# First feed-forward stage's down product in seven-product groups, with the last S5 layer's operators built earlier

## The chip, the cores and the metric

The kernel runs on one core of a Trainium2 chip. The metric is the device time of one execution in microseconds (us), lower is better. TensorE (PE) does the matrix products, VectorE (DVE) and ScalarE (ACT) the elementwise work, GpSimd (POOL) a little arithmetic and the issue of some transfers, SyncE (SP) the issue of most transfers.

## What is computed

A trunk of four layers over one sequence of 512 rows by 1024 columns, all in float32. Each layer adds a mixer and then a feed-forward network (FFN) to the running sum `x`, each on a normalised copy of it:

```python
for layer in range(4):
    h = rmsnorm(x, norm_mix[layer])
    # layers 0 and 3: S5 (a diagonal state space), 1: gated linear attention, 2: differential attention
    x = x + mixer[layer](h)
    h = rmsnorm(x, norm_ffn[layer])
    g, u = split(h @ w_gate_up[layer])          # 1024 x 5632
    x = x + (silu(g) * u) @ w_down[layer]       # 2816 x 1024
return rmsnorm(x, norm_final)
```

Float32 products are made of three passes of a rounded float32 format: each operand is split into a high part and the remainder, and high x high, high x low and low x high are summed.

The S5 layer works with *operators* (small matrices that take 16 inputs of a group into 64 states, and states to outputs) and *phases* (cosines and sines), both computed from the layer's parameters alone. So the last S5 layer's operators and phases can be made at any earlier time. They are: made in pieces beside other work, written ("spilled") to DRAM, and read back in layer 3.

## The kernel before

The order of work is: first S5 layer (`s5_first`, ending in its gate and output products, `s5_glu`), FFN 0, linear attention (`gla`), FFN 1, differential attention (`diff`), FFN 2, last S5 layer (`s5_second`), FFN 3.

**Products.** The FFN's gate and up product (`seven_block`) is done in 11 blocks of 256 hidden columns, each as seven products of half-size matrices in place of eight (Strassen's scheme). The down product has two forms. `gemm_b` is the direct one: for each pair of 128-row weight slices and each of four row tiles it issues three 128x512 matmuls (`mm3`, lines 510 to 512). `seven_down` does four blocks at once with seven half-size products (matmuls at line 384), with more splitting and adding on DVE and ACT. FFN 1, 2 and 3 do their 11 blocks in groups of 4, 4 and 3, the first two by `seven_down`, the last by `gemm_b`. FFN 0 alone does groups of 3, 3, 3 and 2, all four by `gemm_b`.

**Jobs.** `gemm_b` with `jobs=True` calls `job()` after each three matmuls. This advances a Python generator by one step, which emits a few instructions of side work. Their place in the program is tied behind the latest weight split and the latest matmul. In FFN 0 the generator is `s5_spilled`: in eight rounds `kk` = 0 to 7 it loads parameters (`s5_loads`), multiplies complex numbers on DVE (`cross`, lines 1508 to 1510), transposes and multiplies small matrices on PE (`s5_qt` line 1554, `s5_xts` line 1655, `s5_rows` line 1621), copies on ACT, shuffles a map through DRAM (`s5_map`, lines 1637 and 1646), and spills three tiles per round (lines 1777 to 1779). All its transfers go through POOL's queue (`self.dq = nc.gpsimd`). A round takes 17 steps. Its tiles lie in the normalised input's memory, which the other FFNs use as weight slots once the opening is over; FFN 0 therefore has two slots of its own more and only three activation buffers (`na = 3`).

The phases (`s5_phases_spilled`, eight steps a round, DVE and ACT only, and one spill) and small tables for the differential attention (`diff_tables`, 13 steps) are jobs of the linear attention's output product (32 steps) and of the last down groups of FFN 1 (16 steps) and FFN 2 (the rest).

**Order.** Most stages are ordered by a list scheduler that takes instructions in program order where its cost model finds them ready. Some stretches are fixed in program order for all engines: `hand_all()` in `gemm_b` begins one at the last four weight slices of the last product of a stage (the tail), and it lasts until the opening of the next FFN (a plan written out in `ffn`) is over. Weight loads go through SP's queue in order, the accumulating loads ("plus") through POOL's.

**Memory.** The FFN and attention pools reuse the same addresses. A tile's first write waits for everything that used the older tiles at its addresses. `edge` tiles only shift addresses. `gate` in `s5_glu` has a ring of 6 x 2048 bytes per partition at the start of the pool.

Of the kernel before, what the change touches and what calls it, by code (L numbers as in the profile page):

```python
# [22 lines left out]
P = 128  # L23
D = 1024
# [370 lines left out]
class Trunk:  # L395
# [578 lines left out]
    def ffn(self, l, left, after=None, turn=False, aside=None, small=None):  # L974


        jobs = bool(aside or small)
        if small:
            self.calls = 16 if l == 1 else -1
# [4 lines left out]
        with self.tc.tile_pool(name=f"ffn{l}", bufs=1, reuse_waits="tile") as fp:  # L984

            na = 3 if aside else 4
# [6 lines left out]
            slots = [fp.tile([P, 4, 256], F32, name=f"slot{n}") for n in range(SLOTS + 2 * (4 - na))]  # L993
# [11 lines left out]
            halved = () if aside else (0, 1)  # L1005
# [66 lines left out]
            for nb in (4, 4, 3) if na == 4 else (3, 3, 3, 2):  # L1072
# [45 lines left out]
                if small:  # L1118
                    self.place = lambda kk: Slices(*slots[2 * (kk % 2) : 2 * (kk % 2) + 2])
# [6 lines left out]
                for d in range(2):  # L1126
                    tail = 4 if d == 1 and b0 + nb == 11 else 0
                    self.gemm_b(stat, wd, 2 * nb, d * 512, self.add_x(d, nxt, r), k0=2 * b0, tail=tail, jobs=bool(aside) or small and not d,
# [3 lines left out]
                    if small and not d:  # L1132
                        self.closed() if l == 1 else list(self.jobs)
# [5 lines left out]
            list(self.jobs) if l == 0 else None  # L1139
# [572 lines left out]
    def s5_spilled(self, pool, L):  # L1712


        nc = self.nc
        inm = pool.tile([P, 2, 4, 64], F32, name="inmsp")
# [5 lines left out]
        self.spill = [{} for _ in range(8)]  # L1722
        self.dq = nc.gpsimd
        raw = self.s5_loads(pool, L, 0, 4)
# [6 lines left out]
        yield  # L1731
        nxt = operators(0, self.s5_qt(raw[1]))
        for kk in range(8):
# [7 lines left out]
            yield  # L1741
            two()
            if kk < 7:
                raw = self.s5_loads(pool, L, 4 * kk + 4, 4)
            yield
# [4 lines left out]
            yield  # L1750
            q_two()
            yield
            yield
            yield
            if kk == 0:
                yield
                yield
                yield
            both = self.tp("cps")
            if kk < 7:  # L1760
                ps = self.s5_qt(raw[1], both)
# [3 lines left out]
            if kk:  # L1765
                yield
            nc.scalar.copy(inm, xs)
            yield
            if kk:
                yield  # L1770
            self.s5_map(L, 4 * kk, 4, rv, rs, mp, True)
            if kk:
                yield
            if kk < 7:
# [6 lines left out]
            yield  # L1781
# [541 lines left out]
    def s5_glu(self, L, zT, accs, after):  # L2323
# [5 lines left out]
        with self.tc.tile_pool(name=f"s5g_{L}", bufs=1) as p:  # L2329
            for d in range(2):  # L2330
                gate = [None] * NT

                def evac_b(t, ps):
                    gate[t] = p.tile([P, 512], F32, tag="gate", name="gate", bufs=6)
# [30 lines left out]
    def gla(self, l, left, after):  # L2365
# [5 lines left out]
        with self.tc.tile_pool(name="gla", bufs=1, reuse_waits="tile") as p:  # L2371
# [369 lines left out]
    def diff_tables(self):  # L2741
# [8 lines left out]
        p = Slices(self.wp.tile([P, 2048], F32, tag="whl", name="dtab", bufs=5))  # L2750
# [484 lines left out]
    def small(self):  # L3235
        yield from self.diff_tables()
# [53 lines left out]
```

## Time and profile before

| | us |
|---|---|
| median of three runs | 2193.45 (2191.31 to 2194.58) |
| the profiled execution's own time | 2192.53 |
| its span, first to last instruction | 2190.8 |
| PE busy in the span | 2131.8 (97%) |
| DVE busy | 1768.2 (81%) |
| ACT busy | 1198.3 (55%) |
| POOL busy | 383.2 (17%) |
| first S5 layer's gate and output products | 139.0 to 206.75 |
| FFN 0 | 206.75 to 564.83 |
| linear attention's output product | 719.34 to 770.09 |
| FFN 1 | 770.09 to 1102.17 |
| FFN 3 | 1861.20 to 2183.29 |

The stages' limits are the starts of their first matmuls. PE busy is the time in which at least one matmul was under way; a matmul's own time (0.39 us for 128x512) is longer than the spacing of two in a row, since they overlap. PEld is the load of the stationary operand, which overlaps the matmuls too. "POOLq" and "SPq" are the queues from which transfers are issued. An arrow names what ended a wait.

### The profile page before, as it was taken

The page shows a single profiled execution, that of the slowest core. Times are in us where ns is not written, and L with a number is a line of the kernel's source. Part 1 is how long each engine was busy: PE and PEld are TensorE (multiplying, and loading weights), DVE is VectorE, ACT ScalarE, POOL GpSimd, SP SyncE. Part 2 cuts the span into 40 slices and gives each one's busy share as a digit, 9 for nine tenths or more (in the row PEclk, how much of TensorE's full clock was granted, in tenths as well). Part 3 has the DMA queues.
Part 4 walks back from the last instruction along what each step waited for, and adds up shares of the span by engine and source line. Part 5 has one row for each costly group of instructions (what it writes and reads, how often), then busy time and mean ns, then how long its engine had stood idle before and what let it go on. Part 6 is the DMA issues. An engine that isn't in the chain of part 4 may idle for free. (4 is left out here: it accounts for less than half of the span.)

```text
span 2190.8 us, 38556 instructions
## 1 busy us (share of the span) xinstructions
PE 2131.8 (97%) x15241; PEld 1936.7 (88%) x15241; DVE 1768.2 (81%) x2644; ACT 1198.3 (55%) x1874; POOL 383.2 (17%) x486
## 2 busy tenths in 40 slices
PE   6999999999999999999999999999999999999998
PEld 5888989989988899999887888989998888989997
DVE  9965978786887799888785786998987974998985
ACT  8634645444665565455555786654555333655553
POOL 3401151431211111111012231111110000111100
PEclk9999999999999999999999999999999999999999
DMA  4356667774863678986477565998862556799852
GB/s 93 66 176 173 177 164 188 172 185 129 208 161 97 188 189 221 222 202 164 143 218 135 114 156 144 246 241 213 204 165 81 153 153 153 191 228 229 203 141 77
DMA packets 328278, 370.40 MB, mean 169 GB/s; under 512 B 71716, under 2 KB 254144, under 8 KB 327970
## 3 DMA queue, kind: packets, MB, share of 16 engines
q1 hardware_dynamic: 246626, 253.68, 38.0%
q0 software_dynamic: 81472, 114.26, 28.3%
q8 instruction: 120, 1.97, 0.4%
q14 instruction: 60, 0.49, 0.1%
HBM read 333.93 MB, written 18.75 MB: 161 GB/s over the span
## 5 line engine op out<-in xcount | busy, mean ns | idle before, releaser
L482 DVE TENSOR_TENSOR whl<-wst,whl 128x1024 fp32r<-128x1024 f32 x240 | 292.0, 1223 | 143.5 <-ACT whl L474 142.2
L656 PE MATMUL a<-side,whl 128*128 128x256 f32 x3240 | 393.9, 278 | 6.7 <-DVE whl L482 4.2
L656 PEld LDWEIGHTS a<-side,whl 128*128 128x128 f32 x3240 | 380.3, 189 | 9.8 <-DVE whl L482 5.7
L474 ACT CAST whl<-wst 128x1024 fp32r<-128x1024 f32 x240 | 251.2, 1051 | 186.6 <-PE acc L512 79.7
L656 PE MATMUL c<-side,whl 128*128 128x256 f32 x2160 | 260.5, 277 | 1.0 <-DVE whl L482 0.7
L656 PEld LDWEIGHTS c<-side,whl 128*128 128x128 f32 x2160 | 252.5, 188 | 1.5 <-DVE whl L482 1.1
L482 DVE TENSOR_TENSOR whl<-slot,whl 128x1024 fp32r<-128x1024 f32 x132 | 160.7, 1223 | 53.0 <-ACT whl L474 52.7
L474 ACT CAST whl<-slot 128x1024 fp32r<-128x1024 f32 x132 | 138.4, 1052 | 106.4 <-DVE slot L912 46.1
L474 ACT CAST whl<-halves 128x1024 fp32r<-128x1024 f32 x111 | 116.2, 1051 | 85.8 <-DVE halves L912 31.5
L482 DVE TENSOR_TENSOR whl<-halves,whl 128x1024 fp32r<-128x1024 f32 x111 | 135.2, 1222 | 18.9 <-ACT whl L474 18.4
L384 PE MATMUL a<-whl,part 128*128 128x512 f32 x576 | 134.7, 389 | 0.0
L656 PE MATMUL a<-sides,whl 128*128 128x256 f32 x1080 | 132.2, 278 | 1.0 <-DVE whl L482 1.0
L656 PE MATMUL d<-sides,whl 128*128 128x256 f32 x1080 | 131.3, 278 | 0.0
L656 PEld LDWEIGHTS a<-sides,whl 128*128 128x128 f32 x1080 | 128.0, 188 | 2.0 <-DVE whl L482 1.2
L656 PEld LDWEIGHTS d<-sides,whl 128*128 128x128 f32 x1080 | 127.6, 188 | 0.2 <-DVE whl L482 0.2
L384 PEld LDWEIGHTS a<-whl,part 128*128 128x128 f32 x576 | 107.6, 188 | 22.3 <-issue 0.3
L510 PE MATMUL acc<-whl,act 128*128 128x512 f32 x320 | 126.4, 395 | 0.9 <-ACT whl L474 0.4
L512 PE MATMUL acc<-whl,act 128*128 128x512 f32 x320 | 125.1, 391 | 0.0
L511 PE MATMUL acc<-whl,act 128*128 128x512 f32 x320 | 125.0, 390 | 0.0
L837 POOL DMA_DIRECT2D wst<-in_ffn_w_gate_up_dram x44 | 57.0, 1296 | 256.4 <-DVE whl L482 66.8
L510 PE MATMUL acc<-whl,zT 128*128 128x512 f32 x192 | 75.5, 393 | 0.0
L511 PE MATMUL acc<-whl,zT 128*128 128x512 f32 x192 | 74.9, 390 | 0.0
(610 smaller groups left out, 4463.0 us busy)
## 6 DMA issues: line engine op xcount, KB each, us to landing
wst<-in_ffn_w_gate_up_dram SPq DMA_DIRECT2D x88, 512.0 KB, 6.4
wst<-in_ffn_w_down_dram SPq DMA_DIRECT2D x70, 512.0 KB, 5.0
slot<-in_ffn_w_gate_up_dram SPq DMA_DIRECT2D x63, 512.0 KB, 5.7
halves<-in_ffn_w_gate_up_dram SPq DMA_DIRECT2D x45, 512.0 KB, 5.7
wst<-in_ffn_w_gate_up_dram POOLq DMA_DIRECT2D x44, 512.0 KB, 7.2
wst<-in_s_w_glu_dram SPq DMA_DIRECT2D x32, 512.0 KB, 4.5
slot<-in_ffn_w_gate_up_dram POOLq DMA_DIRECT2D x24, 512.0 KB, 8.4
wst<-in_diff_w_qkv_dram SPq DMA_DIRECT2D x22, 512.0 KB, 4.9
```

Of the source, the lines that this page charges most:

```text
L384: self.tr.last["mm"] = self.tr.nc.tensor.matmul(banks[t][:], row(y, k, t), hl[:, z, k % 2], start=first and not (k or n), stop=k == 3 and ...
L474: self.last["high"] = self.nc.scalar.copy(hl[:, 0], w[:])
L482: self.last["low"] = self.nc.vector.tensor_tensor(hl[:, 1], w[:], hl[:, 0].bitcast(F32), op=ALU.subtract)
L510: mm(out, lh, rh, start=first, stop=False)
L511: mm(out, lh, rl, start=False, stop=False)
L512: self.last["mm"] = mm(out, ll, rh, start=False, stop=last)
L656: mm(o, *two, start=first and not (j or k or n), stop=k == 3 and n == 2, skip_group_check=True,)
L837: nc.gpsimd.dma_start(w[:], left.quarter(*plus, b), accum_op=ALU.add)
```

## The change

FFN 0 takes the form of the other three: groups of 4, 4 and 3 blocks, four activation buffers, the first two groups by `seven_down`, and the normalised input's memory as weight slots. It has no operator jobs. Its last group has 16 steps of phase jobs (rounds 0 and 1) beside the first half of its down product.

The operators' rounds 0 to 5 become jobs of the three products in the first S5 layer's `s5_glu` (32, 32 and 16 possible steps), in a tile `made` behind an edge of 12352 bytes; one `gate` tile is taken first, so that the ring lies ahead of the edge. Rounds 6 and 7 become jobs of the first half of the linear attention's output product, in two side tiles that its blocks have finished with. In its second half come 8 steps of phases (round 2), in the third side tile. FFN 1's last group gets the tables and then phases (29 steps, rounds 3 and 4), FFN 2's the remaining rounds.

`s5_spilled` itself: a round takes 9 steps, five empty steps come before the first, and its loads, the write of the map and half of the map's reads move from POOL's queue to SP's. With `jobs=True` in `s5_glu` and in the attention's second half, `gemm_b` also emits each weight load and split one pair of slices ahead.

```diff
-    def ffn(self, l, left, after=None, turn=False, aside=None, small=None):
+    def ffn(self, l, left, after=None, turn=False, small=None, calls=-1):
...
-            na = 3 if aside else 4
+            na = 4
...
-            halved = () if aside else (0, 1)
+            halved = (0, 1)
...
-            if aside:
-                self.jobs = aside(Slices(left.whole, left.g))
-            else:
+            if True:
                 slots[:] = [F[0], F[1], slots[0], F[2], left.g[:].rearrange("p (k n) -> p k n", n=256), F[3]] + slots[1:]
...
-            for nb in (4, 4, 3) if na == 4 else (3, 3, 3, 2):
+            for nb in (4, 4, 3):
...
                 if small:
-                    self.place = lambda kk: Slices(*slots[2 * (kk % 2) : 2 * (kk % 2) + 2])
+                    self.place = lambda kk: Slices(own[kk % 2], own[2][:, 2 * (kk % 2) : 2 * (kk % 2) + 2])
+                    self.jobs, self.calls = small, calls
...
     def s5_spilled(self, pool, L, kks):
...
-        self.dq = nc.gpsimd
-        raw = self.s5_loads(pool, L, 0, 4)
+        self.dq = nc.sync
+        raw = self.s5_loads(pool, L, 4 * kks[0], 4)
...
-        yield
-        nxt = operators(0, self.s5_qt(raw[1]))
-        for kk in range(8):
+        for _ in range(5):
+            yield
+        nxt = operators(kks[0], self.s5_qt(raw[1]))
+        for kk in kks:
...
# s5_glu
+            gates = [p.tile([P, 512], F32, tag="gate", name="gate", bufs=6)]
+            if L == 0:
+                self.edge(p, 12352)
+                self.spill = [{} for _ in range(8)]
+                self.jobs = self.s5_spilled(lambda: Slices(p.tile([P, 3712], F32, name="made")), 1, (0, 1, 2, 3, 4, 5))
...
-                    self.gemm_b(stat, wg, KT, D + d * 512, evac_b)
+                    self.gemm_b(stat, wg, KT, D + d * 512, evac_b, jobs=not L)
...
-                    self.gemm_b(stat, wg, KT, d * 512, evac_a, tail=4 if d else 0, ahead=ahead, behind=behind)
+                    self.gemm_b(stat, wg, KT, d * 512, evac_a, tail=4 if d else 0, ahead=ahead, behind=behind, jobs=not L)
             self.last.pop("gate")
+            list(self.jobs)
...
# gla
-            self.jobs = self.small()
-            self.calls = 32
-            self.place = lambda kk: Slices(self.wp.tile([P, 2048], F32, tag="whl", name="phases", bufs=5))
+            self.jobs = self.s5_spilled(lambda: Slices(room("side1", "made"), room("side2", "made")), 1, (6, 7))
+            self.calls = -1
+            spare = room("side3", "made")
             for d in range(2):
                 self.gemm_b(
-                    so, wo, KT, d * 512, self.add_x(d, nxt), tail=4 if d else 0, between=() if d else late, jobs=not d,
+                    so, wo, KT, d * 512, self.add_x(d, nxt), tail=4 if d else 0, between=() if d else late, jobs=True,
                     ahead=(lambda: (nxt.ahead(2), nxt.total("3"))) if d else None,
                 )
-                self.closed()
+                list(self.jobs) if d == 0 else self.closed()
+                self.jobs, self.calls = tables, 8
+                self.place = lambda kk: Slices(spare)
...
# run
-        left = self.ffn(0, left, i["norm_mix"][1], aside=lambda fp: self.s5_spilled(fp, 1))
-        left = self.gla(1, left, i["norm_ffn"][1])
-        left = self.ffn(1, left, i["norm_mix"][2], small=True)
+        tables = self.s5_phases_spilled(1)
+        left = self.ffn(0, left, i["norm_mix"][1], small=tables, calls=16)
+        left = self.gla(1, left, i["norm_ffn"][1], tables)
+        left = self.ffn(1, left, i["norm_mix"][2], small=chain(self.diff_tables(), tables), calls=29)
```

More of the change, by code (lines that the diff above doesn't have):

```diff
@@ L992, in ffn @@
                 lent = room()
-            slots = [fp.tile([P, 4, 256], F32, name=f"slot{n}") for n in range(SLOTS + 2 * (4 - na))]
+            slots = [fp.tile([P, 4, 256], F32, name=f"slot{n}") for n in range(SLOTS)]
+            own = list(slots)
             if not glued:
@@ L1127, in ffn @@
                     tail = 4 if d == 1 and b0 + nb == 11 else 0
-                    self.gemm_b(stat, wd, 2 * nb, d * 512, self.add_x(d, nxt, r), k0=2 * b0, tail=tail, jobs=bool(aside) or small and not d,
+                    self.gemm_b(stat, wd, 2 * nb, d * 512, self.add_x(d, nxt, r), k0=2 * b0, tail=tail, jobs=not d and bool(small),
                                 behind=None if d or l == 0 else dict(self.last),
@@ L1721, in s5_spilled @@
         nc.gpsimd.memset(rs[:, :, :48], 0.0)
-        self.spill = [{} for _ in range(8)]
-        self.dq = nc.gpsimd
-        raw = self.s5_loads(pool, L, 0, 4)
+        self.dq = nc.sync
+        raw = self.s5_loads(pool, L, 4 * kks[0], 4)
+        end = kks[-1]
         def operators(kk, ps):
@@ L2363, in gla_ahead, with gla @@
         )
-    def gla(self, l, left, after):
+    def gla(self, l, left, after, tables):
         nc, i = self.nc, self.i
@@ L2749, in diff_tables @@
         yield
-        p = Slices(self.wp.tile([P, 2048], F32, tag="whl", name="dtab", bufs=5))
+        p = self.place(1)
         if True:
```

39 lines of the change are left out of this document (9 added, 30 removed).

## The prediction

> **What bounds the kernel now.** I read the page's totals first, then stretches of the trace stage by stage, then single stretches of PE in order of time, then waits.
>
> ```profile
> span 2190.8 us, 38556 instructions
> PE 2131.8 (97%) x15241; PEld 1936.7 (88%) x15241; DVE 1768.2 (81%) x2644; ACT 1198.3 (55%) x1874; POOL 383.2 (17%) x486
> PEclk9999999999999999999999999999999999999999
> ```
>
> PE is covered for 97% of the span at the full granted clock, so time changes where PE's own stream changes, or where a hole opens in it. The stretches below show, for each stage that the change touches and for FFN 1 and FFN 3 as measures, its length and the busy time of PE, PEld, DVE, ACT and POOL.
>
> ```profile
> 139.00:206.75 67.75, 67.75 (x314) 56.05 (x313) 32.73 (x40) 25.70 (x40) 5.16 (x4) 1.00 0.63 167
> 206.75:564.83 358.08, 356.05 (x2867) 327.19 (x2866) 287.15 (x437) 183.25 (x291) 104.82 (x153) 1.00 0.67 173
> ...
> 719.34:770.09 50.75, 49.86 (x240) 40.44 (x239) 38.48 (x101) 30.76 (x60) 6.84 (x7) 1.00 0.69 188
> 770.09:1102.17 332.08, 326.80 (x2371) 306.75 (x2370) 285.22 (x332) 185.31 (x236) 40.63 (x34) 0.99 0.74 187
> ...
> 1861.20:2183.29 322.09, 322.07 (x2343) 302.44 (x2341) 270.49 (x302) 172.11 (x212) 40.20 (x34) 1.00 0.70 177
> ```
>
> FFN 3 already has the form that FFN 0 gets, with the same written opening, and runs it in 322.09 us without a hole; FFN 0 takes 358.08 with 2.03 us of idle PE. FFN 1, of the same form with another opening and with jobs, takes 332.08, of which 5.28 is idle. In the first S5 layer's gate and output products PE has no idle time, but DVE works only 32.73 of 67.75 us.
>
> The spacing of 128x512 matmuls shows whether a busy PE is a full one. These are the first and last of 23 rows without a break in the first S5 layer's products:
>
> ```profile
> 194.79 0.39 PE L511 MATMUL acc<-whl,zT 128*128 128x512 f32 x1
> ...
> 199.78 0.39 PE L512 MATMUL acc<-whl,zT 128*128 128x512 f32 x1
> ```
>
> 22 intervals in 4.99 us are 0.227 each, and that is the price of one matmul taken out of the stream.
>
> **The change part by part. FFN 0's products.** A direct product of 16 of the 22 weight slices is 16 x 4 x 3 x 2 = 384 matmuls. Seven half-size products make 336 of it, which is what FFN 3 issues at line 384:
>
> ```profile
> 1861.00:2183.00 322.00, 76.67 (x336) 62.83 (x336) 1.00 0.70 177
> ```
>
> 76.67 against 384 x 0.227 = 87.2 saves 10.5 us. The extra splits and sums on DVE (270.49 of 322.09 in FFN 3) are hidden by PE there.
>
> **The rule against the row.** The Trainium skill (Perfetto Trace Analysis, Identifying the Most-Contended Engine) says that matmul busy time is no good measure for TensorE and that the busy share of weight loads should be used. By it PE is an 88% engine, and a removed matmul would be worth its weight load rather than its spacing:
>
> ```profile
> L511 PEld LDWEIGHTS acc<-whl,act 128*128 128x128 f32 x320 | 60.1, 188 | 11.7
> ```
>
> 48 x 0.188 would be 9.0 us by that rule and 48 x 0.227 = 10.9 by the spacing, so either way the term stays near 10; the spacing without breaks decides here.
>
> **FFN 0's jobs on PE.** They leave FFN 0 and come back elsewhere. A steady round is one block of 28 small products, in records:
>
> ```profile
> 377.42 0.39 PE L512 MATMUL acc<-whl,act 128*128 128x512 f32 x1
> 377.74 0.66 PE L1554 MATMUL cps<-ident,halves 128*64 128x128 f32 x8
> 378.33 1.15 PE L1655 MATMUL xps<-ident,halves 64*64 64x64 f32 x32
> 379.41 0.45 PE L1621 MATMUL cps<-halves 128*32 128x64 f32 x16
> 379.79 0.51 PE L510 MATMUL acc<-whl,act 128*128 128x512 f32 x1
> ...
> 391.75 0.66 PE L1554 MATMUL cps<-ident,halves 128*64 128x128 f32 x8
> ```
>
> From 377.42 to 379.79 less one spacing is 2.14 us a round. Without its eight line 1554 records (the first at 377.74, the next group at 378.33: 0.6) it is 1.55, and these alone cost 0.67 with the switch. Rounds 0 to 5 in a row are 0.67 + 5 x 2.14 + 1.55 = 12.9 us; rounds 6 and 7 are 0.67 + 2.14 + 1.55 = 4.4.
>
> **FFN 0 afterwards.** FFN 3's 322.1 plus the transposes for the attention's input, which FFN 3 does not have (27 records more, at 0.35 us for four):
>
> ```profile
> 564.48 0.60 PE L117 MATMUL tp<-ident,hh 128*128 128x128 f32 x4
> 564.83 3.08 PE L656 MATMUL a<-sides,whl 128*128 128x256 f32 x24
> ```
>
> That is 324.5. FFN 1 shows what is late in such a last group: the next norm's gain, which can be loaded only when its memory is no longer a weight slot. PE waits behind DVE, and DVE behind that load:
>
> ```profile
> PE tp L117 <- DVE hh L95: 1.9, 1, 1.9
> DVE hh L95 <- DMA gain<-in_norm_mix_dram: 1.8, 1, 1.8
> ```
>
> FFN 0 now uses the gain's memory as a slot in the same way, so I add 2 and take 326.5; the bounds are 324.5 and FFN 1's 332.1. The term is 326.5 - 358.1 = -31.6 (-33.6 to -26.0). The phase steps beside that group use DVE and ACT only; PE covers them as it does in FFN 1.
>
> **The first S5 layer's products.** +12.9 on PE, plus holes. DVE must do the `cross` work:
>
> ```profile
> 206.75:564.83 358.08, 15.68 (x48) 0.00 (x0) 1.00 0.67 173
> 206.75:564.83 358.08, 15.66 (x48) 0.00 (x0) 1.00 0.67 173
> 206.75:564.83 358.08, 15.89 (x48) 0.00 (x0) 1.00 0.67 173
> ```
>
> The three lines (1508 to 1510) make 47.2 us for eight rounds, 5.9 each. Six are 35.4; with 32.7 that is 68 in 67.75 + 12.9 = 80.7 us, 84%, so DVE holds. A round has 9 steps of 0.68 us (three matmuls) plus 2.14: 8.3 us. What a hole costs shows at the first full round in FFN 0, where PE came to operands that were not ready:
>
> ```profile
> 278.86 0.39 PE L512 MATMUL acc<-whl,act 128*128 128x512 f32 x1
> 279.18 0.66 PE L1554 MATMUL cps<-ident,halves 128*64 128x128 f32 x8
> 279.77 1.50 PE L1655 MATMUL xps<-ident,halves 64*64 64x64 f32 x32
> 281.61 0.27 PE L1621 MATMUL cps<-halves 128*32 128x64 f32 x2 [0.34 <-DVE halves L1510]
> 281.81 0.50 PE L510 MATMUL acc<-whl,act 128*128 128x512 f32 x1
> 282.54 0.45 PE L1621 MATMUL cps<-halves 128*32 128x64 f32 x14 [0.22 <-DVE halves L1510]
> 282.92 0.50 PE L511 MATMUL acc<-whl,act 128*128 128x512 f32 x1
> ```
>
> 4.06 less two spacings is 3.61, 1.5 above a steady round. The scheduler can let the main matmuls pass a late block, so holes in every round are the upper bound (6 x 1.5 = 9), none the lower; I take 2. FFN 0's first weight loads stand behind the last round's transfers on SP. They are issued from here on now, 31 us ahead of FFN 0:
>
> ```profile
> 175.76 0.50 SPq L834 DMA_DIRECT2D slot<-in_ffn_w_gate_up_dram  x1
> ```
>
> Six rounds of 8.3 after five empty steps of 0.68 end 53 us into the 81, so the loads can still start 28 us ahead and cost nothing.
>
> **The queues.** Per round eight or nine transfers move from POOL to SP, ahead of or between weight loads. On POOL they waited in order for PE and ACT:
>
> ```profile
> POOL halves L1521 <- PE cps L1554: 23.8, 2, 13.9
> POOL rd L1637 <- ACT halves L1635: 18.4, 2, 17.2
> ```
>
> On SP such a wait holds back weight loads, and behind them splits and PE. In this stage SP itself now waits 39.3 us for free staging buffers, so loads run well ahead:
>
> ```profile
> SPq L463 <- DVE whl L482: 39.3, 12, 10.4
> ```
>
> I price it at nothing within that lead; beyond it, it is the second rival's.
>
> The Trainium skill (DMA: Bandwidth & Descriptors, Issuing engines are not separate DMA queues) holds that the issuing engine decides only the time to initiate a transfer. By that rule the move to SP could neither hold back weights nor help, and the 3 us of holes taken in these two stages would be nought: -13.8 in place of -10.8. POOL's rows above show 42 us of waiting in order on the issuing queue, which the rule leaves out, so I keep the 3.
>
> **The attention's output product.** +4.4 on PE. The phases that go, and the two rounds that come (11.8 us of DVE), are about equal loads on DVE (38.48 of 50.75). Holes: 1 (-1 to 4, since 0.9 us of the 50.75 is idle already). The third side tile ends 64 bytes above the start of FFN 1's first weight slot (2 x 8192 + 128 + 3 x 8192 against 5 x 8192 + 64), so that slot's load, and in fixed order on SP all behind it, waits for the phase spill. Now it starts here:
>
> ```profile
> 746.74 0.58 SPq L834 DMA_DIRECT2D slot<-in_ffn_w_gate_up_dram  x1
> ...
> 767.08 1.28 POOL L837 DMA_DIRECT2D wst<-in_ffn_w_gate_up_dram  x1 [3.00 <-DMA wst<-in_ffn_w_gate_up_dram]
> ...
> 789.12 1.05 ACT L474 CAST whl<-wst 128x1024 fp32r<-128x1024 f32 x1
> ```
>
> Eight steps of 0.68 after the half's start, then the spill, make it about 9 us later against FFN 1's start. The last accumulating load, now issued 22 us ahead of its split, keeps 13 less its own flight, so it is covered; with FFN 1's tables (DVE and ACT work) I put 0.5 (-1 to 3) on FFN 1.
>
> **The sum.** -31.6 + 12.9 + 2 + 4.4 + 1 + 0.5 = -10.8; with all lower bounds -18.3, with all upper ones +7.3 (-26.0 + 12.9 + 9 + 4.4 + 4 + 3). The profiled execution's own time is 2192.53 (span plus 1.7), so it would become 2181.7. The median of the runs is 0.9 above it: 2182.6.
>
> **The rivals.**
>
> *FFN 0 runs like FFN 1.* The splits of the seven-product groups hold PE as at FFN 1's start. For it: FFN 1's 5.28 us of idle PE, DVE at 86% there. Against: FFN 3 shares FFN 0's opening and has none. 332.1 in place of 326.5: -5.2, 2188.3.
>
> *Holes in every round.* The loads, the map and the weights queue on SP, and each of eight rounds stalls PE by the 1.5 us of the first one: 12 in place of 3, -1.8, 2191.7. For it: half the steps between a load and its use. Against: the lead of the weights.
>
> *The rounds overrun (slower).* From a stage's tail on, the order is fixed, so leftover jobs must be done first. The rounds have 80 steps x 0.68 + 12.9 = 67.3 us; after five empty steps (3.4), six rounds fit if each takes at most 10.65 us. In FFN 0 a round takes 14.0 (378 to 392 in the rows above). If it were its chain of loads, DVE and copies that takes so long, and not the 17 steps, six need 87.4: 20.1 us of idle PE in place of the 2, +7.3, 2200.7. Against: 17 x 0.68 + 2.14 is 13.7, so the steps alone explain the 14.0.
>
> **How the numbers follow.** Forecast 0.60, centre 2182.6, own range 2176 to 2188; FFN 1's way 0.15; holes 0.15; overrun 0.10. The range of 2176 to 2194 takes in the first three but for their ends. About 0.2% (4.4 us) can be told from no change. Faster by more: 0.59 + 0.09 + 0.03 = 0.71; within: 0.01 + 0.06 + 0.10 + 0.01 = 0.18; slower: 0.02 + 0.09 = 0.11.
>
> **What would show it.** Right: FFN 0's stretch near 326 us with 336 line 384 records; the first S5 layer's stretch near 83 and the attention's near 56, with line 1554, 1655 and 1621 records there; FFN 1 within 1 us of 332. Wrong: waits of PE on transfers or DVE at lines 1554 or 1621, a hole ahead of the S5 stage's last matmuls, SP's weight loads late, or FFN 0 over 330.

## The result, and the profile after

The changed kernel takes 2180.03 us in the median (2179.01 to 2180.94), the kernel before 2192.61 (2191.31 to 2194.58). The ratio is 0.9942, with a 95% interval of 0.9925 to 0.9959: 12.6 us or 0.6% faster. The prediction was 2182.6 us. The profiled spans differ by 11.6 us, from 2190.8 to 2179.2. The first two rows of the page after:

```profile
span 2179.2 us, 38598 instructions
PE 2121.5 (97%) x15193; PEld 1925.2 (88%) x15193; DVE 1796.3 (82%) x2675; ACT 1215.6 (56%) x1886; POOL 357.7 (16%) x427
```

PE's share is what it was; PE has 48 records and 10.3 us of busy time less. Where the time went is read stage by stage. These are stretches of the kernel after (length, then busy time of PE, PEld, DVE, ACT and POOL with their instructions, granted clock, DMA share, GB/s):

```profile
139.00:225.41 86.41, 84.45 (x650) 65.85 (x649) 61.73 (x156) 40.57 (x101) 29.14 (x46) 1.00 0.72 190
225.41:550.65 325.24, 325.21 (x2372) 305.30 (x2370) 283.81 (x332) 186.50 (x237) 46.22 (x39) 1.00 0.83 207
705.10:760.38 55.28, 54.24 (x351) 43.45 (x349) 36.78 (x78) 27.91 (x63) 13.84 (x19) 1.00 0.73 187
...
1357.41:1690.20 332.79, 326.32 (x2341) 303.40 (x2340) 290.16 (x358) 183.56 (x239) 47.56 (x46) 1.00 0.76 191
...
1690.20:1849.70 159.50, 156.09 (x958) 137.69 (x957) 113.69 (x158) 52.92 (x85) 9.16 (x14) 0.99 0.58 155
```

Two stretches of the kernel before that the prediction did not need, FFN 2 and the second S5 layer:

```profile
1367.51:1698.90 331.39, 325.34 (x2342) 303.08 (x2341) 288.75 (x356) 182.63 (x237) 46.73 (x45) 1.00 0.76 192
...
1698.90:1861.20 162.30, 157.38 (x959) 139.12 (x957) 114.60 (x161) 53.65 (x87) 9.82 (x14) 0.98 0.57 154
```

| stage | before, us | after, us | difference | forecast |
|---|---|---|---|---|
| first S5 layer's gate and output products | 67.75 | 86.41 | +18.66 | +14.9 |
| FFN 0 | 358.08 | 325.24 | -32.84 | -31.6 |
| attention's output product | 50.75 | 55.28 | +4.53 | +5.4 |
| FFN 1 | 332.08 | 332.85 | +0.77 | +0.5 |
| FFN 2 | 331.39 | 332.79 | +1.40 | 0 |
| second S5 layer | 162.30 | 159.50 | -2.80 | 0 |
| all others | 888.4 | 887.1 | -1.28 | 0 |

The sum is -11.56 us. FFN 0 now runs without a hole (325.24 us, 325.21 of them PE). The S5 stage costs 3.8 us more than forecast, and two stages that the prediction did not look at moved. Most of "all others" is the differential attention (265.34 to 264.18), which took 265.2 us in the second profiles of both kernels, so I do not count it to the change.

**The S5 stage.** PE idles for 2 us there, and 1.64 of it is one hole:

```profile
174.02 0.39 PE L512 MATMUL acc<-whl,zT 128*128 128x512 f32 x1
176.05 0.66 PE L1549 MATMUL cps<-ident,made 128*64 128x128 f32 x8 [1.64 <-DMA made<-in_s_c_re_dram]
```

Line 1549 is line 1554 of before. SP's queue in order of time shows why its operand is late:

```profile
168.64 1.74 SPq L1641 DMA_DIRECT2D made<-rd  x4
...
171.99 0.48 SPq L1516 DMA_DIRECT2D made<-in_s_c_re_dram  x1
```

The load of c stands behind the map transfers of the round before, which wait on SP for other transfers to land (SP's waits in this stage; us, times, longest):

```profile
SPq L1641 <- DMA map<-made: 16.0, 4, 5.6
SPq L1641 <- DMA rd<-made: 10.4, 5, 4.2
```

The other surplus is in the PE blocks. In FFN 0 a steady round's 28 products stood in one block. Here the scheduler cuts the six rounds into 15 pieces. One of the smallest, two records of line 1616 (1621 before):

```profile
149.09 0.40 PE L510 MATMUL acc<-whl,zT 128*128 128x512 f32 x1
149.42 0.30 PE L1616 MATMUL cps<-made 128*32 128x64 f32 x2
149.65 0.50 PE L511 MATMUL acc<-whl,zT 128*128 128x512 f32 x1
149.98 0.39 PE L512 MATMUL acc<-whl,zT 128*128 128x512 f32 x1
```

From 149.09 to 149.65 is 0.56 us, 0.33 more than a spacing of 0.227, for two records; and the next spacing, 149.65 to 149.98, is 0.33 instead of 0.227. So a return from small products to the main stream costs another 0.1 us behind the block, where my price for a block (up to the next main matmul) did not look. The four transposes of line 117, which have the main matmuls' own 128*128 form, cost the same behind them (168.78 to 169.10 is 0.32), but they start 0.23 us behind the main matmul at 168.20, where a piece starts 0.33 behind the one at 149.09:

```profile
168.43 0.60 PE L117 MATMUL tp<-ident,hh 128*128 128x128 f32 x4
168.78 0.48 PE L510 MATMUL acc<-whl,zT 128*128 128x512 f32 x1
169.10 0.40 PE L511 MATMUL acc<-whl,zT 128*128 128x512 f32 x1
```

### The profile page after: what moved, and what is told of

It is laid out like the page before. It is cut to its first block, busy times and chain, and to the rows that moved or that the text cites. A ratio compares the mean times of both kernels' runs of the same rounds, so it can differ in the third digit from the quotient of the medians.

```text
span 2179.2 us, 38598 instructions
## 1 busy us (share of the span) xinstructions
PE 2121.5 (97%) x15193; PEld 1925.2 (88%) x15193; DVE 1796.3 (82%) x2675; ACT 1215.6 (56%) x1886; POOL 357.7 (16%) x427
## 5 line engine op out<-in xcount | busy, mean ns | idle before, releaser
L474 ACT CAST whl<-halves 128x1024 fp32r<-128x1024 f32 x143 | 149.7, 1051 | 106.7 <-DVE halves L912 42.0
L482 DVE TENSOR_TENSOR whl<-halves,whl 128x1024 fp32r<-128x1024 f32 x143 | 174.3, 1222 | 22.3 <-ACT whl L474 21.9
L384 PE MATMUL a<-whl,part 128*128 128x512 f32 x768 | 179.6, 389 | 0.0
L384 PEld LDWEIGHTS a<-whl,part 128*128 128x128 f32 x768 | 143.4, 188 | 29.8 <-issue 0.5
L482 DVE TENSOR_TENSOR whl<-slot,whl 128x1024 fp32r<-128x1024 f32 x112 | 136.3, 1223 | 38.7 <-ACT whl L474 38.5
L384 PE MATMUL c<-whl,part 128*128 128x512 f32 x384 | 89.6, 389 | 0.0
L384 PEld LDWEIGHTS c<-whl,part 128*128 128x128 f32 x384 | 72.1, 188 | 15.0
L510 PE MATMUL acc<-whl,act 128*128 128x512 f32 x192 | 76.4, 399 | 1.7 <-DVE x L638 1.7
L1150 ACT CAST part<-raw 128x1024 fp32r<-128x1024 f32 x48 | 50.5, 1054 | 48.2 <-PE c L384 13.3
L510 PE MATMUL acc<-whl,zT 128*128 128x512 f32 x192 | 76.7, 399 | 0.0
```

Of the source, the lines that this page charges most:

```text
L384: self.tr.last["mm"] = self.tr.nc.tensor.matmul(banks[t][:], row(y, k, t), hl[:, z, k % 2], start=first and not (k or n), stop=k == 3 and ...
L474: self.last["high"] = self.nc.scalar.copy(hl[:, 0], w[:])
L482: self.last["low"] = self.nc.vector.tensor_tensor(hl[:, 1], w[:], hl[:, 0].bitcast(F32), op=ALU.subtract)
L510: mm(out, lh, rh, start=first, stop=False)
L1150: self.last["part high"] = nc.scalar.copy(o[:, 0, ks], y)
```

## The experiments

One execution can stand up to 1.9 us ahead of another at 139 us. In this section the S5 stage is therefore measured from the same matmul on, the 284th main one ahead of FFN 0: 67.66 and 67.65 us in two profiles of the kernel before, 86.31 and 85.35 in two of the kernel after.

### The kernel before and the kernel after, once more

> The kernel before, once more, for a second profile. The stages that the change doesn't touch differed between the two first profiles: diff attention 265.3 to 264.2, FFN 2 331.4 to 332.8, the second S5 layer 162.3 to 159.5 us. Theory (these differences are the granted clock's low stretches, which fall elsewhere in each execution): the second S5 layer is near 159 us here too, with a granted clock of 1.00 at its start. Rival (the change reaches them): it is 162 us again with a granted clock below 0.90 at its start.

> The changed kernel, once more, as the measure for the runs beside it on the same chip. Theory: the stages that the change touches repeat within 0.3 us (S5 stage 86.4, FFN 0 324.9, attention's output 54.9), the rest moves by up to 2 us with the granted clock; 2180 us. Rival (the stages touched are themselves different from execution to execution): one of them is over 1 us away.

The kernel before took 2193.13 us in this one run. Its second S5 layer was as long as the first time (162.72 us), and again began at a low clock:

```profile
1699.10:1709.10 10.00, 7.71 (x52) 7.28 (x50) 5.45 (x12) 6.10 (x13) 4.63 (x10) 0.83 0.87 195
```

The kernel after took 2179.51 us (2176.54 to 2179.92), ratio 0.9935 (0.9920 to 0.9950). Its second S5 layer took 158.52 us. My theory for that stage falls: the 3 us are no accident of the clock, the change reaches them. FFN 2 took 330.9 us in the kernel before and 333.1 in the kernel after, so its +1.4 repeats as well. Of the stages touched, FFN 0 (325.5 against 325.2 us) and the attention's output (55.32 against 55.28) repeat in the kernel after; the S5 stage differs by 0.96 us, because the load of c came a little earlier. In the kernel before FFN 0 took 360.4 us this time, 2.3 more than in the first profile: its granted clock was 0.83 from 255 to 265 us. The differences below are taken from the first profile.

### FFN 0's products direct again

```diff
-            halved = (0, 1)
+            halved = (0, 1) if l else ()
...
-                if small:
+                if small and b0 == 8:
```

> The changed kernel, but FFN 0's first two down groups are direct products again (groups of 4, 4 and 3 blocks, without jobs in the first two); the moved rounds stay where the change put them. Theory (PE's stream sets FFN 0's length, and the 336 half-size matmuls save 10.5 us against the 384 of 0.227 us): FFN 0 goes from 325.2 to about 335.7 us, the whole to about 2190.5 us, idle PE in FFN 0 stays under 0.5 us. Rival (moving the jobs out and their switches is what shortened FFN 0; the products only exchange PE time for splits): FFN 0 stays within 2 us of 325.2, the whole at about 2180 to 2182 us.

2195.61 us (2191.50 to 2198.78), ratio to the kernel before 1.0017 (1.0008 to 1.0027). FFN 0's stretch:

```profile
226.76:565.80 339.04, 337.02 (x2420) 314.49 (x2418) 247.10 (x295) 169.21 (x225) 32.72 (x27) 1.00 0.66 168
```

It is 13.8 us longer than after the change: 11.8 us of PE's busy time for 48 records more, where I had forecast 10.5, and 2.0 us of idle time, 1.6 of it some 52 us into the stage, where the kernel before idles too and PE waits mostly for weights that are not split yet (1.2 us). The rival falls. The rest of FFN 0's gain is the other comparison: 358.08 before against 339.04 here, 19.0 us, for 447 records of jobs (2867 against 2420). My price for these was 17.2 (0.67 + 7 x 2.14 + 1.55); the returns to the main stream were left out of it. So FFN 0's -32.84 is 13.8 of products and 19.0 of jobs; the 19.0 also hold the other grouping of the blocks, which no run separates. The jobs cost 18.66 + 4.53 = 23.2 us in the two stages that took them, so moving them alone gains nothing. The whole differs from the changed kernel by 15.6 us; what is above 13.8 lies in stages that the edit does not touch.

### The c loads a round earlier

```diff
             if kk < end:
                 ps = self.s5_qt(raw[1], both)
+                if kk + 1 < end:
+                    raw[1] = load_c(kk + 2)
...
             two()
             if kk < end:
-                raw = self.s5_loads(pool, L, 4 * kk + 4, 4)
+                raw[0] = load_b(kk + 1)
```

> The changed kernel with the c loads of a round issued a round earlier, right behind the transposes that free their buffer, ahead of the map's transfers on SP. Theory (the 1.6 us hole of the S5 stage comes from the c_re load standing behind four map reads on SP): PE's waits on c_re go, the S5 stage is 84.3 to 84.8 us, the whole about 2178.4 us. Rival (the round's DVE chain is as late as the load, so another wait takes the place): the stage stays at 86 us, PE waits for DVE at the small products.

2180.53 us (2176.47 to 2183.66), ratio 0.9954 (0.9937 to 0.9970), which cannot be told from the kernel after. The stretch can:

```profile
139.22:223.50 84.28, 84.28 (x650) 65.70 (x648) 61.77 (x156) 40.44 (x100) 28.38 (x46) 1.00 0.74 193
```

PE has no idle time left in the stage. In none of the five profiles with the early load does PE wait for c. But the length alone is no proof: in the run on the place of the phase scratch, below, the stage has the code of the changed kernel, and it took 84.28 us there too. What differs is when the load of c went out behind the 284th main matmul: 30.2 us there, without a hole, against 31.8 in the second profile of the kernel after (1.0 us of waiting) and 32.9 in the first (1.6). So the theory holds in this form: with the load behind the map transfers on SP, the hole is as long as these happen to take, 0 to 1.9 us in four profiles.

What remains, 84.28 - 67.66 = 16.6 us, is the price of six rounds on PE without any wait, against my 12.9. Adding up, for each of the 15 pieces, the time between the main matmuls on its two sides less one spacing gives 14.7 (without 0.5 for transposes that the kernel before pays too); 15 returns of 0.11 add 1.7.

### Fewer pieces

```diff
             q_two()
             yield
+            yield
+            yield
             both = self.tp("cps")
```

> The early c loads, and two more empty steps a round ahead of a round's PE block (71 of 80 steps). By the written order the six rounds then stand in the PE stream in 11 pieces instead of 15. Theory (a piece costs its small products, about 0.2 us for the switch and 0.11 us on the next main matmul): the S5 stage falls from 84.5 by 4 x 0.3 to about 83.3 us; the FFN's first weight load starts 8 us later, still over 10 us ahead of FFN 0, which stays at 324.9 us. Rival (the pieces cost nothing by themselves, the small products alone take the 16.7 us): the S5 stage stays at 84.5 us. Second rival (a lead of 11 us is too short for FFN 0): FFN 0 takes 327 us.

2176.87 us (2175.46 to 2177.25), ratio 0.9925 (0.9910 to 0.9939).

```profile
140.44:223.41 82.97, 82.97 (x649) 65.82 (x648) 62.22 (x156) 40.95 (x100) 28.18 (x45) 1.00 0.68 187
```

The same 168 small products (336 records) in 11 pieces instead of 15 take 1.31 us less: 0.33 a piece, as expected (0.24 by the last experiment's profile, where the stage with the same 11 pieces took 83.31 us). FFN 0 stayed at 325.4 us with its first weight load 15.2 us ahead (208.23 against 223.41). This is the fastest version of this study; its interval overlaps that of the changed kernel beside it (0.9920 to 0.9950), so only the stage shows the gain.

The Trainium skill (TensorEngine Tiling (Array Packing), Key Properties) says that a change of the tiling mode, not just of the tile, drains TensorE. The rows of the pieces show fewer rows and columns in use (64*64, 128*64 or 128*32 in place of 128*128); the tiling mode itself is not in the trace. The trace agrees in direction: a piece costs about 0.3 us, and it starts 0.1 us later behind a main matmul than most of the 128*128 transposes do. The 0.1 behind the return, which these transposes cost as well, needs another cause, and no run here shows which.

A third empty step, with the block written behind the round's last DVE step, makes 10 pieces:

> The early c loads, three empty steps a round ahead of the PE block (77 of 80 steps), and the block written behind the round's last DVE step: 10 pieces in place of 15. Theory (a piece less is worth about 0.33 us, as two empty steps showed: 84.3 to 83.0 us from the same main matmul on; FFN 0's weights still have a lead of about 11 us): the S5 stage is 82.6 us by that measure, FFN 0 stays at 325 us, the whole is 2176 to 2177 us, 3 us below the changed kernel. Rival (the lead is what is short, as with all eight rounds at 8.2 us): FFN 0 takes 326 to 328 us with PE waiting for weight splits near its start, and the whole is 2178 to 2180 us.

2177.21 us (2175.13 to 2180.25), ratio 0.9935 (0.9923 to 0.9948). The S5 stage took 83.38 us, not 82.6: a new hole of 0.7 us ahead of line 1616 took what the piece gave. PE's busy time there was 82.65 us, 0.32 less than with 11 pieces. FFN 0 took 325.20 us without a hole, and its first weight load was issued at 213.13, 11.0 us ahead of FFN 0 at 224.10. So 11 us are lead enough, and that rival falls.

### All eight rounds beside the S5 products

```diff
-                self.jobs = self.s5_spilled(..., 1, (0, 1, 2, 3, 4, 5))
+                self.jobs = self.s5_spilled(..., 1, tuple(range(8)))
...
-            self.jobs = self.s5_spilled(..., 1, (6, 7))
+            self.jobs = iter(())
```

> The changed kernel with all eight rounds beside the first S5 layer's products (77 of 80 steps) and none beside the attention's output product. Theory (a round's pace is its nine steps, 8.3 us, and its cost its PE block): the S5 stage grows from 86.4 by 2 x 2.14 and two more cut blocks to 91 to 92 us, the attention's output stage falls from 55.3 to about 51 us, the whole stays at 2180 to 2181 us. Rival (a round's chain of loads, DVE and copies takes 10.65 us or more): the rounds end about 17 us after the last step, PE idles for that long ahead of the stage's tail, the whole is about 2197 us.

2185.38 us (2179.25 to 2185.94), ratio 0.9968 (0.9955 to 0.9981). The S5 stage and FFN 0:

```profile
139.47:232.51 93.04, 89.27 (x762) 69.17 (x760) 71.87 (x194) 45.47 (x120) 33.75 (x57) 1.00 0.61 166
232.51:561.04 328.53, 326.55 (x2372) 306.05 (x2370) 283.89 (x332) 186.59 (x237) 49.91 (x41) 1.00 0.86 213
```

No overrun: the last block on PE begins at 214.3, 18 us ahead of the stage's end, so the slower case that the prediction priced at 2200.7 falls. The attention's output, at 50.80 us, gives back 4.5 as expected. But the S5 stage has 3.8 us of holes, 3.6 of them waits for c, and FFN 0 loses 3.3 us. Its first weight load now stands behind the last round's transfers on SP and is issued at 224.30, 8.2 us ahead of FFN 0; PE then waits three times, 2.0 us, for splits 15 to 20 us into FFN 0; the other 1.3 us are more busy time of PE (326.55 against 325.21), which I did not trace. The lead that I had counted as cover ends between 11.0 and 8.2 us.

### The queues

The first run puts the rounds' small loads and map transfers back on POOL; the second has all eight rounds beside the S5 products, early c loads, and the map transfers of the last two rounds on POOL.

```diff
-        self.dq = nc.sync
+        self.dq = nc.gpsimd
```

> The changed kernel with the rounds' small loads, map write and half of the map reads issued by POOL, as before the change, in place of SP. By the rule that the issuing engine only sets the time to initiate a transfer nothing changes: 2180.0 us, the S5 stage 86.4 us, the wait of 1.6 us of PE on c_re stays. Theory (an instruction waits in order on its issuing queue): SP's waits of 16.0 and 10.4 us at the map's transfers go, POOL gets waits of that size at the same lines; the hole ahead of the c transposes changes its place and size (0 to 6 us over the stage); the whole 2178 to 2185 us.

> All eight rounds beside the first S5 layer's products, with the early c loads, and with the map transfers of the last two rounds issued by POOL. With all eight on SP FFN 0's first weight load was issued 8.2 us ahead of FFN 0, and FFN 0 took 328.2 us with 2.0 us of idle PE. Theory (that load stood in order behind the last rounds' map transfers on SP): it is issued 20 us or more ahead of FFN 0, which is back at 325 us; the S5 stage is 88.5 to 89.5 us without holes, the attention's output stage 50.4 us; the whole about 2178 us. Rival (the load waits for the memory of the rounds, or FFN 0 loses its time to something else): it is issued under 10 us ahead and FFN 0 takes 328 us again.

On POOL: 2184.18 us (2181.07 to 2185.99), ratio 0.9965 (0.9952 to 0.9978). The S5 stage took 88.38 us, 2 to 3 more than in the two profiles of the kernel after, but only 0.7 more than in the run with direct products (87.72), where its code was the same as in these. Waits of POOL, then of PE, in that stage:

```profile
POOL made L1641 <- DMA map<-made: 7.0, 2, 5.2
```

```profile
PE cps L1549 <- DMA made<-in_s_c_re_dram: 2.4, 3, 1.5
PE cps L1549 <- DMA made<-in_s_c_im_dram: 0.4, 1, 0.4
```

SP's waits at the map's transfers are gone, POOL has such waits instead, and PE waits for c four times in place of once. The scheduler also cut the blocks otherwise (13 pieces), so this run does not separate the two. The second run shows the queue's part in the lead: 2182.82 us (2179.34 to 2189.07), ratio 0.9953 (0.9937 to 0.9969), with the S5 stage at 89.02 us as expected and the first weight load 19.7 us ahead, as expected; yet FFN 0 took 335.99 us in the profiled execution. Neither theory had that. POOL's queue around FFN 0's start:

```profile
236.52 0.56 POOL L1780 DMA_DIRECT2D map<-made  x1 [4.42 <-DMA made<-rd]
237.07 2.71 POOL L837 DMA_DIRECT2D lent<-in_ffn_w_gate_up_dram  x2
```

The last of these rows, the first accumulating weight load of FFN 0, goes out 9.1 us after FFN 0's start at 228.01. In the kernel after it goes out 13.1 us ahead of the start at 225.41:

```profile
212.29 1.34 POOL L837 DMA_DIRECT2D lent<-in_ffn_w_gate_up_dram  x1 [1.12 <-DMA lent<-in_ffn_w_gate_up_dram]
```

Here it stands behind the last map, ACT's split waits 10.7 us for it, and PE behind ACT:

```profile
246.35 0.80 PE L656 MATMUL c<-side,whl 128*128 128x256 f32 x2 [6.57 <-ACT whl L474]
```

Of the 10.7 us that FFN 0 is longer than 325.3, 7.06 are idle time of PE; the rest is busy time at a low clock around and behind that hole:

```profile
240.00:250.00 10.00, 3.19 (x13) 2.89 (x14) 3.39 (x3) 4.56 (x6) 4.77 (x4) 0.63 1.18 186
```

The profiled execution was the longest of the five (2189.07 us, 6.3 above their median), so the others lost less here or elsewhere.

The Trainium skill's rule (DMA: Bandwidth & Descriptors, Issuing engines are not separate DMA queues), that issuing from several engines saves only the usually small time to initiate a transfer, leaves out what this trace shows: 22 us of delay against FFN 0's start came from what was ahead on the issuing queue. So the lead is one of two queues, and in these runs the one that took the last round's transfers held back its weights.

### The place of the phase scratch

The second profile of the kernel before left a question: what of the change reaches the second S5 layer? SP, DVE and PE of the kernel before, in order of time around FFN 2's end:

```profile
1689.41 0.34 SPq L594 DMA_DIRECT2D gain<-in_norm_mix_dram  x1
...
1693.80 3.10 DVE L258 TENSOR_TENSOR hu<-x,gain 128x512 f32<-128x512 f32 x5 [2.12 <-DMA gain<-in_norm_mix_dram]
...
1703.80 0.33 PE L289 MATMUL rt<-ident,Rt 128*128 128x128 f32 x1 [1.88 <-DVE Rt L281]
```

The gain tile's own rows in that stretch hold something that is no gain (each: duration least, median, most in ns; first and last start):

```profile
L1695 DVE SCALAR_TENSOR_TENSOR gain<-mrow,s5flo,gain x8: 346/347/347, 1672.1 to 1686.5; 128x128 f32<-128x128 f32 x8
```

The phases used the gain's memory as scratch until 1688, so the gain could be loaded only then. Five products `hu` queued up behind it on DVE, the last add of `x` came at 1701.15, 2.3 us after the next stage's first matmul, and PE waited for the norm that follows. In the kernel after, where the change has put the scratch in the FFN's own first three slots, the same load:

```profile
1619.14 0.34 SPq L594 DMA_DIRECT2D gain<-in_norm_mix_dram  x1
```

The experiment undoes this part alone:

```diff
-                    self.place = lambda kk: Slices(own[kk % 2], own[2][:, 2 * (kk % 2) : 2 * (kk % 2) + 2])
+                    self.place = lambda kk: Slices(*slots[2 * (kk % 2) : 2 * (kk % 2) + 2])
```

> The changed kernel with one part undone: in the FFNs the phase scratch stands again in the first entries of the renewed slot list, two of which are freed buffers (the gain's memory among them), in place of the FFN's own first three slots. Theory (the scratch in the gain's memory held the next gain's load until the last phase step, and that is what makes the second S5 layer 3.2 us shorter after the change, 162.5 to 159.0): the gain loads are issued some 60 us later, the second S5 layer takes 162 to 163 us again with DVE waiting for the gain, and FFN 0, whose phases now lie in the gain's memory too, gets the wait of 2 us that the prediction had put there (326.5 to 327.5 us); the whole 2184 to 2186 us. Rival (something else of the change shortens the second S5 layer): it stays at 158.5 to 159.5 us, the whole at 2180 us.

2189.02 us (2185.88 to 2194.11), ratio 0.9986 (0.9976 to 0.9995). FFN 0, the attention up to its output product, the beginning of the second S5 layer and that layer as a whole:

```profile
223.21:550.87 327.66, 325.62 (x2372) 305.60 (x2370) 283.93 (x332) 186.82 (x237) 46.81 (x39) 1.00 0.79 200
550.87:708.28 157.41, 151.60 (x1224) 138.08 (x1222) 133.57 (x214) 96.48 (x164) 23.92 (x31) 1.00 0.61 152
...
1694.09:1704.09 10.00, 7.77 (x53) 7.25 (x51) 5.37 (x12) 6.21 (x13) 4.64 (x10) 0.83 0.73 193
1694.09:1856.63 162.54, 157.62 (x959) 139.22 (x957) 114.62 (x160) 53.61 (x87) 9.83 (x14) 0.98 0.57 153
```

The second S5 layer is back at 162.5 us, with the low clock at its start. FFN 0 gets the very wait that the prediction had put there:

```profile
527.03 0.35 SPq L594 DMA_DIRECT2D gain<-in_norm_mix_dram  x1
...
532.21 1.90 DVE L95 TENSOR_TENSOR hh<-x,gain 128x512 f32<-128x512 f32 x3 [2.31 <-DMA gain<-in_norm_mix_dram]
...
532.96 1.26 PE L117 MATMUL tp<-ident,hh 128*128 128x128 f32 x8 [2.04 <-DVE hh L95]
```

The theory holds, and the whole is dearer than I expected by some 4 us: the attention up to its output product takes 157.41 instead of 154.45. There the late gain load also stands ahead of the attention's weight loads in SP's written order; I did not test that by itself. By medians this one line is worth 9 us of the 12.6 (by the profiled spans 7.2, 2186.4 against 2179.2). FFN 0's 2.4 and the attention's 3.0 of it are costs that the kernel before does not have (154.51 us for that part of the attention).

The early gain has a price, in FFN 2. DVE near the end of FFN 2 in the kernel after, then in the kernel before:

```profile
1672.56 1.28 DVE L258 TENSOR_TENSOR hu<-x,gain 128x512 f32<-128x512 f32 x2
1674.73 0.50 DVE L1686 TENSOR_SCALAR slot<-slot 128x512 f32<-128x512 f32 x1 [0.89 <-ACT slot L1684]
1675.15 0.73 DVE L638 SCALAR_TENSOR_TENSOR x<-acc,rturned,x 128x512 f32<-128x512 f32 x1
```

```profile
1681.55 2.72 DVE L638 SCALAR_TENSOR_TENSOR x<-acc,rturned,x 128x512 f32<-128x512 f32 x4
```

Before, the four adds that free PE's accumulators (line 638) stand together. With the gain there early, two products with it and a phase step that waits for ACT come ahead of the third add, and PE waits 1.30 us for it. PE's waits for these adds at line 510 come to 1.4 to 2.6 us in the nine profiles with the new place and three phase rounds in FFN 2, to 0.4 and 0.8 in the kernel before and to 0.2 in this run, whose FFN 2 took 330.84 us.

### Three phase rounds in FFN 0

```diff
-        left = self.ffn(0, ..., small=tables, calls=16)
+        left = self.ffn(0, ..., small=tables, calls=24)
```

> The early c loads and two empty steps a round, and in the FFNs three of the eight phase rounds in FFN 0's last group (24 steps in place of 16), so that FFN 2 has two left in place of three. Theory (FFN 2 takes 332.8 to 333.2 us after the change against 330.9 to 331.4 before because its third phase round puts DVE steps ahead of the adds that free PE's accumulators): FFN 2 takes 331 to 331.5 us again, FFN 0 stays within 0.5 us of 325.0 since PE has covered the phases there, the whole is 2174.5 to 2175.5 us. Rival (a third round in FFN 0 costs there what it saves in FFN 2, or FFN 2's time has another cause): FFN 0 takes 326.5 us or more, or FFN 2 stays at 333 us; the whole 2176.5 to 2178 us.

2178.98 us (2177.94 to 2180.87), ratio 0.9948 (0.9935 to 0.9962). FFN 0 and FFN 2:

```profile
222.56:550.66 328.10, 325.67 (x2372) 305.44 (x2370) 286.62 (x342) 190.07 (x244) 47.69 (x40) 1.00 0.82 206
1356.71:1688.31 331.60, 325.58 (x2342) 302.80 (x2340) 287.23 (x348) 180.17 (x232) 46.86 (x45) 1.00 0.76 190
```

Theory and rival are each right in one stage. FFN 2 falls from 333.15 (in the version that this one is built on) to 331.60, and PE's wait for the adds there to 0.3 us. But the theory's reason is wrong: the kernel before has the same three phase rounds in FFN 2 (30 instructions on DVE and 21 on ACT in both kernels), so the change added none. What it cost there is the order on DVE shown above, and taking a round away mends that, as the old place of the scratch does. The stage's length alone would not show it, since it was 331.15 to 333.64 us in the nine profiles. FFN 0 rises by 2.7. DVE near its end:

```profile
530.48 0.43 DVE L1686 TENSOR_SCALAR slot<-slot 128x512 f32<-128x512 f32 x1 [2.48 <-ACT slot L1684]
```

A phase step waits 2.48 us for ACT, the product for the next norm waits in order behind it, and PE waits 2.3 us for that product. "Hidden by PE" holds for two phase rounds in FFN 0 and not for three.

## Why the prediction was right, and where it was wrong

**FFN 0: right, with one wrong term.** "Near 326" was 325.24, with the 336 records of line 384 at 76.61 us. The products were worth 13.8 instead of 10.5, the jobs 19.0 instead of 17.2. The step "FFN 0 now uses the gain's memory as a slot in the same way, so I add 2" failed. I had read FFN 1's late gain as the price of a weight slot. The tile's own rows in the kernel before show that the last split out of it was at 1026.6, and that the phases read it at 1074.5 (the gain's load went out at 1075.27):

```profile
L482 DVE TENSOR_TENSOR whl<-gain,whl x1: 1219/1219/1219, 1026.6 to 1026.6; 128x1024 fp32r<-128x1024 f32 x1
...
L1702 ACT ACTIVATE halves<-gain,halfpi x1: 727/727/727, 1074.5 to 1074.5; 128x512 f32<-128x512 f32 x1
```

The changed line that moves the scratch stood in the diff, and the prediction did not weigh it. With the old place the 2 us were there (327.66), so the size was right and the cause wrong. In FFN 1 the gain now comes at 1016.50 instead of 1075.27, and PE still waits 1.9 us at the same place, where DVE now has a split of the next stage's weights (1.23 us at 1086.09) ahead of the product that PE waits for: the wait that the prediction quoted had a second cause ready behind the first.

**The S5 stage: right in kind, 3.8 us short.** The term "six rounds in a row are 12.9 us" is 16.6 without any hole: it took whole blocks, and a block's price up to the next matmul. The written order cut them into 15 pieces, and each return adds 0.11 us. The "2" for holes was 2.0, at the place named (line 1554, on a transfer), and that is luck: with the same code it was 1.0 in the second profile and none in the run on the scratch's place.

**The price of a product.** The prediction weighed 9.0 us by the weight loads against 10.9 by the spacing for 48 matmuls. The runs show 11.8 us of PE's busy time, 0.246 each, so the spacing was nearer. The section of the Trainium skill cited there (Perfetto Trace Analysis, Identifying the Most-Contended Engine) judges how close a kernel is to roofline and states no price for a matmul; that was my inference.

**The lead.** The prediction had the first weight load of FFN 0 28 us ahead; it was 19.3 (206.09). It cost nothing, as forecast, and the experiments put the limit between 11.0 and 8.2 us.

**The attention's output: right** (+4.53 against +5.4). The claim that FFN 1's first slot load would come "about 9 us later against FFN 1's start" was wrong. The phase spill and that load in the kernel after:

```profile
726.38 0.54 POOL L1774 DMA_DIRECT2D cs<-made  x1 [0.92 <-ACT made L1697]
...
733.51 0.43 SPq L834 DMA_DIRECT2D slot<-in_ffn_w_gate_up_dram  x1
```

The spill is done early, since the phase steps run ahead of their place in the program, and the load goes out 26.9 us ahead of FFN 1 (23.4 before).

**What was not forecast at all:** the second S5 layer (-2.8 and -4.2 in the two pairs of profiles) by the place of the scratch, and FFN 2 (+1.4 and +2.2) by the order on DVE that the early gain brings. These and the S5 stage's +3.8 against FFN 0's -1.2 and the attention's -0.9 nearly cancel. The total is closer than its terms, and in part that is luck: with the scratch at its old place the whole takes 2189.02 us, outside the prediction's own range of 2176 to 2188.

**The rivals.** "FFN 0 runs like FFN 1" fell: 0.03 us idle. "Holes in every round" fell: one hole of 1.64 and one of 0.3 in six rounds. "The rounds overrun" fell, even with eight.

## What to carry to other kernels

When a diff moves a scratch tile, ask which loads waited for the old place: the rows of the tile, not of the engine, show who held it, and the wait may appear in a stage that the diff does not name. A small product put into a stream of large matmuls costs its switch and its return, so count pieces as well as products, and check in the written order how many there are. Before you name a cause, look whether the kernel before has it too: the third phase round of FFN 2 was there all along. A queue that takes over transfers which wait holds back whatever stands behind them; measure how many microseconds of lead it had left before using it as cover.

## What was not expected of the hardware

A piece of small products between 128x512 matmuls costs about 0.3 us beyond the products (15 to 11 pieces: 84.28 to 82.97 us), and the first spacing after its return is 0.33 us in place of 0.227; that spacing is 0.32 after four 128*128 transposes too. A PE hole of 1.8 to 1.9 us at the start of the second S5 layer came with a granted clock of 0.83 for the 10 us around it in three of three profiles with the late gain, and 1.00 in the kernel after, whose first 10 us of that layer are:

```profile
1690.20:1700.20 10.00, 9.01 (x74) 8.33 (x73) 7.43 (x14) 6.26 (x11) 3.97 (x10) 1.00 0.92 222
```

The layer was 2.8 to 4.2 us longer with the hole. A second low stretch some 23 us into the layer (0.83 over 10 us) does not follow the change: the first profile of the kernel after has it and the second has not, and that layer took 159.50 and 158.52 us. That the hole lowers the clock is likely from these rows and from FFN 0 with all eight rounds (0.63 around a hole of 6.57 us), but no run here changed the one without the other.
